# Two transformer blocks on one core: middle chunks of four gated feed-forwards with the weights stationary, and three tiles padded

## Chip, core and metric

The kernel runs on one core of a Trainium2 chip. The metric is the device time of one execution in microseconds (us).

## What is computed

Two blocks work on 256 tokens of width 1024, in float32. The first has an mLSTM mixer and a convolutional gated feed-forward. The second has two layers of three sublayers each: a gated feed-forward, a mixer (gated linear attention, then latent attention), and another gated feed-forward. So block 2 has four gated feed-forwards, each inside a norm before, a norm after and a residual:

```python
D_MODEL = 1024
D_FF = 2816

def swiglu(h, w_gu, w_down):
    gate, up = jnp.split(h @ w_gu, 2, axis=-1)
    return (jax.nn.silu(gate) * up) @ w_down

def sublayer(x, shift, scale, gate, g_pre, g_post, fn, res_weight):
    h = rmsnorm_2(x, g_pre) * (1 + scale[:, None, :]) + shift[:, None, :]
    return x + res_weight * gate[:, None, :] * rmsnorm_2(fn(h), g_post)
```

The vectors `shift`, `scale` and `gate` come from products of a condition vector with large matrices (GEMV), which the kernel does on VectorE.

## The kernel before

All 256 tokens stay on the core: `x` holds two tiles of 128 tokens (a and b). Every matrix product is done in three matmuls. A float32 number is split into a high part (`whi`, `u_hi`, `hh`) and the rest (`wlo`, `u_lo`, `hl`), and `mm3` adds high x high, high x low and low x high into PSUM (L233 to L235). The activations that enter a product, `u_hi` and `u_lo`, have features on partitions, [128, 8, 256].

A *unit* is 512 KB of weights: `unit` loads it into one of 5 `raw` buffers from SyncE's queue, ScalarE casts the high part (L219) and VectorE subtracts to get the low part (L220); 8 places hold each of the two, and some units go to spare places of the arena (`wA`, `wB`, `wC`, `wU`).

A gated feed-forward is cut into 11 chunks of 256 features. `up(c, t)` handles chunk c for token tile t: `as_proj` keeps the activations stationary and streams the weights, 8 steps of three matmuls with 512 columns (256 of the gate, 256 of the value), so its result has tokens on partitions. ScalarE takes Silu (`sg`, L927), VectorE multiplies (`h_`, L929), TensorE transposes the product in two pieces (`pt2`, L932), and `hilo` splits it into `hh` (ScalarE, L228) and `hl` (VectorE, L229). `down(c, t)` multiplies that by two units of the second matrix, 12 matmuls of 512 columns into accumulators of the tile. The four units of an up serve both token tiles. Elsewhere, in the convolutional stage and for keys and queries, `ws_proj` does it the other way round: weights stationary, both token tiles streamed as 256 columns.

What stands in which order: `FFN_ORDER` gives the ups and downs of each feed-forward, one string for each of the four. After each up, `site()` issues as many GEMV slices (`gjunk`, L239, one load of 512 KB each) as the table `FILL` says. A scheduler then orders the instructions of each engine; `urgent` and `pin_b` move the norms between stages ahead and tie units behind them. `modulated` builds the input of a stage out of `xn`: 4 transposes into one PSUM place, scale and shift (`u`, L341 on VectorE for one half, ScalarE for the other), then `u_hi` and `u_lo`.

Tiles of a pool lie one behind another in SBUF. `cols` has 422 floats, 1688 bytes, and the tiles `u_hi` and `u_lo` that follow begin 32 bytes past a multiple of 64; so does one of the arena's places, which follows a tile of 8224 bytes.

Of the kernel before, what the change touches and what calls it, by code (L numbers as in the profile page):

```python
# [18 lines left out]
NF = FF // 128  # L19
# [5 lines left out]
def _cols_layout():  # L25
# [14 lines left out]
# GEMV slices of the modulation vectors issued at each point of the program  # L40
# [7 lines left out]
# chunks of the gated feed-forwards in order: up (u) and down (d), chunk, token tile (a, b)  # L48
FFN_ORDER = (
# [8 lines left out]
)  # L58
# per norm between two stages and token tile: its urgency; weight units and GEMV slices that queue behind it
# [6 lines left out]
# spare places (arena tags) for the weight units of a stage  # L66
# [17 lines left out]
# stages: steps in order  # L84
# [10 lines left out]
def kernel(ctx: ExitStack, tc: tile.TileContext, a: dict, out: bass.AP):  # L95
# [24 lines left out]
    # ---------------------------------------------------------------- constants  # L120
# [12 lines left out]
    cols = const.tile([128, NCOLS], F32, name="cols")  # L133
    nc.sync.dma_start(out=cols, in_=a["cols"])
# [12 lines left out]
    # split activations, features on partitions  # L147
# [3 lines left out]
    def second():  # L151
        """a second stream of split activations: context, then input of the shared keys and values"""
        return [ar.tile([128, 8, 256], F32R, name=f"v{i}", tag=f"U{i}") for i in range(2)]
# [8 lines left out]
    # ---------------------------------------------------------------- helpers  # L162
# [7 lines left out]
    def behind(op, first):  # L170
        """issue op after an earlier instruction of its engine"""
        tc.add_manual_dep(op.ins, first.ins.name, mybir.DependencyInfo(
            mybir.DependencyClass.NoSync, mybir.DependencyReason.DATA), reason="behind a chain")
# [3 lines left out]
    def pin(n, k=0):  # L177
        """the next n weight units queue behind the latest norm"""
        m = dict(mark)
        if k == 1:  # L180
            m["ms"], m["nr"] = m["ehi"], m["elo"]
        elif k == 2:
            m["nr"] = m["elo"]
        elif k == 4:
            m["ms"], m["nr"] = m["xa"], m["xn0"]
        elif k == 3:
            m["ms"] = m["ehi"]
        pins.extend([m] * n)
        return m
# [12 lines left out]
    def ahead(stage, srcs):  # L202
        """the first weight units of the next stage, loaded before their turn"""
        for i, (slot, src) in enumerate(zip("ABC", srcs)):
            early[stage, i] = unit(src, slot)
# [72 lines left out]
    def rsqrt_half(hv, n=1):  # L278
        """hv [128, n] -> 1/sqrt(2 hv): seed from the exponent bits, then Newton steps"""
# [6 lines left out]
        if n == 1:  # L286
            # a step of third order (1.875 - 2.5 t + 1.5 t^2, t = hv y^2), then Newton's
            k = 1.5 ** 0.5
            V.tensor_scalar(out=w[:, 2:3], in0=hv, scalar1=k, scalar2=None, op0=ALU.mult)
            V.scalar_tensor_tensor(out=w[:, 0:1], in0=y, scalar=w[:, 2:3], in1=y, op0=ALU.mult, op1=ALU.mult)  # L290
            V.scalar_tensor_tensor(out=w[:, 1:2], in0=w[:, 0:1], scalar=2.5 / k, in1=w[:, 0:1], op0=ALU.subtract, op1=ALU.mult)
            V.scalar_tensor_tensor(out=r[:, 0:1], in0=w[:, 1:2], scalar=1.875, in1=y, op0=ALU.add, op1=ALU.mult)
            V.scalar_tensor_tensor(out=w[:, 3:4], in0=r[:, 0:1], scalar=hv, in1=r[:, 0:1], op0=ALU.mult, op1=ALU.mult)
            mark["nr"] = V.scalar_tensor_tensor(out=r[:, 1:2], in0=w[:, 3:4], scalar=1.5, in1=r[:, 0:1], op0=ALU.subtract,
                                                op1=ALU.mult, reverse0=True)
            return r[:, 1:2]
# [7 lines left out]
    def mean_square(src, dst, width):  # L304
        """dst [128, 1] = sum(src^2) / (2 width) over the free axis"""
        junk = wk.tile([128, 512], BF16, name="ajunk", tag="ajunk", bufs=1)
        mark["ms"] = S.activation(out=junk[:, :src.shape[-1]], in_=src, func=AF.Square, scale=float(2 * width) ** -0.5, accum_out=dst)  # L307

    def rms_r2(parts, width=D):
        """1/rms over the one or two parts of a row"""  # L310
# [22 lines left out]
    def modulated(xn, gs, sh, uh, ul):  # L333
        """normalised xn [128 tok, 1024] -> split xn * gs + sh, features on partitions"""
# [27 lines left out]
    def t_hilo(src, t):  # L362
        """src [128 tok, 1024] -> u_hi/u_lo[:, :, t]"""
# [5 lines left out]
    def row_of(c):  # L369
        """[128, 8] columns -> [128, 1024] row on every partition"""  # L370
# [21 lines left out]
    def ws_proj(ps, w, uh, ul, nk=8):  # L392
        """weights stationary: ps[128 cols, tokens] = W^T u"""
# [5 lines left out]
    def as_proj(ps, units, n, uh, ul, t):  # L399
        """activations stationary: ps[128 tokens of tile t, n] = u W; units carry 8 k-tiles in order"""  # L400
# [8 lines left out]
    def wo_proj(src, fin, slots=(None,) * 8):  # L409
        """u @ W [1024, 1024], one token tile after the other"""  # L410
# [14 lines left out]
    # ---------------------------------------------------------------- modulation vectors, in order of use  # L425
# [38 lines left out]
    # ================================================================ block 1  # L464
    def cond_rows():
        """c_1 and c_ctx after Silu, on every partition"""
# [8 lines left out]
    def start():  # L475
        """modulated context and latents, keys and gates, one feature tile after the other"""
        b1 = const.tile([128, 8], F32, name="b1")
# [15 lines left out]
        def features(h):  # L493
            """half of the normalised features, on partitions"""
# [33 lines left out]
        def vectors(f):  # L528
            """scale and shift of feature tile f, for context and latents"""
# [21 lines left out]
        def keys(f):  # L551
            """modulated features, their part of the keys and gates"""
# [37 lines left out]
    def mlstm():  # L590
# [4 lines left out]
        # gates, rows: i fwd 0.., i bwd 32.., f fwd 64.., f bwd 96..  # L595
# [53 lines left out]
        # queries, features on partitions  # L649
# [7 lines left out]
        # values and output gates, tokens on partitions  # L657
        vv = [ar.tile([128, 2, H, 257], F32, name=f"vt{i}", tag="BC"[i]) for i in range(2)]
# [22 lines left out]
        # attention  # L681
# [67 lines left out]
    # ---------------------------------------------------------------- conv glu  # L749
    def conv_glu(fin):  # L750
# [9 lines left out]
        def group():  # L760
            """the first feature tiles of gate and value, one token tile after the other"""
# [9 lines left out]
        def tail_val(t):  # L771
            """values of the last feature tiles for token tile t, features on partitions"""
# [122 lines left out]
    # ================================================================ block 2  # L895
# [15 lines left out]
    def swiglu(l, j, after, nxt, hooks):  # L911
        s_ = 0 if j == 0 else 2
        seq = [(e[0], int(e[1:-1]), "ab".index(e[-1])) for e in FFN_ORDER[l * 2 + j].split()]
        W, Wd, hT = {}, {}, {}
# [4 lines left out]

        def up(c, t):  # L920
            if c not in W:
                W[c] = [first(("ffn", l, j), c * 4 + q, a["gu"][l * 2 + j, c, q],
                              EXTRA[c * 4 + q] if c * 4 + q < FFN_FIRST[l * 2 + j] else fs[q] if c == NC - 1 else None) for q in range(4)]
# [13 lines left out]
        def down(c, t):  # L937
            hh, hl = hT.pop((c, t))
# [4 lines left out]
            for k, h in ([(0, 0), (1, 0), (0, 1), (1, 1)] if last else [(0, 0), (0, 1), (1, 0), (1, 1)]):  # L943
                hi, lo = Wd[c][k]
                s = slice(h * 512, h * 512 + 512)
                mm3(acc[t][h], hh[:, k, :], hl[:, k, :], hi[:, s], lo[:, s], cnt[t] == 0 and k == 0, last and k == 1)
# [23 lines left out]
    def gla():  # L970
# [13 lines left out]
        def vr(i, t):  # L984
            """values (i < 2) and output gates, tokens on partitions"""
# [13 lines left out]
        def gates():  # L999
            """cumulative log decay of each chunk"""  # L1000
# [26 lines left out]
        def kq(src, h):  # L1027
            """keys and queries, features on partitions"""
# [107 lines left out]
    def rope(src, dst, tokens, rp):  # L1136
        """src [128, g, tokens] projected pairs of halves -> dst rotated; rp [128, 256] of PSUM"""
# [10 lines left out]
    def mla_u(t, xn):  # L1148
        """modulated input of the shared keys and values, kept until mla_kv"""
# [5 lines left out]
    def mla_latent():  # L1155
        """rotated part of the shared keys, latent of keys and values"""
# [27 lines left out]
    def mla_kn():  # L1184
        """shared keys"""
# [10 lines left out]
    def mla_v():  # L1196
        """shared values"""
# [12 lines left out]
    def mla_mix():  # L1210
# [32 lines left out]
        def latent(t):  # L1243
            """normalised latent of the queries"""
# [16 lines left out]
        def queries(t):  # L1261
            """queries of token tile t, features on partitions: pairs of rotated parts, then heads"""
# [64 lines left out]
def _layout(inp):  # L1327
# [75 lines left out]
    o["gu"] = con(gu.transpose(0, 5, 1, 3, 2, 4, 6)).reshape(4, NC, 4, 128, 1024)  # L1403
# [58 lines left out]
```

## Time and profile before

| what | value |
|---|---|
| median of 3 timed runs | 1444.93 us (1439.31 to 1447.36) |
| profiled execution, span | 1444.4 us |
| TensorE busy | 1395.5 us (97%), 7017 matmuls |
| weight loads busy | 1142.3 us (79%) |
| VectorE busy | 1118.1 us (77%) |
| ScalarE busy | 718.2 us (50%) |
| moved by DMA | 340.06 MB, mean 235 GB/s |

The profiled execution has no timing of its own beside its span, first to last instruction; the median of the timed runs is 0.5 us above it. Busy times overlap between engines. The end of a matmul is modelled in the profile and overlaps with the next one, so the distance between two starts tells what a matmul costs, not its recorded duration.

### The profile page before, as it was taken

Reading aid. Unit: us, or ns where it says so; the run is one execution under the profiler, and the core shown is the slowest. Engines: PE = TensorE matmul, PEld = TensorE weight load, DVE = VectorE, ACT = ScalarE, POOL = GpSimd, SP = SyncE. Lnnn points to the kernel's source line nnn. Section 1 sums busy time; section 2 is a strip of 40 time slices with the busy share of each in tenths; the row PEclk is TensorE's granted clock in tenths of the full one; section 3 lists DMA queues with packets and bytes.
Section 4 is the critical chain, followed back from the end, with each engine's and each line's share of the span. In section 5 each row is a group of like instructions: output and inputs, shape, how many; then the busy total and the mean of one; then the engine's idle time right before and its main releaser. Section 6 shows DMA issues by size and latency. Waiting matters only on the chain.

```text
span 1444.4 us, 19726 instructions
## 1 busy us (share of the span) xinstructions
PE 1395.5 (97%) x7017; PEld 1142.3 (79%) x7017; DVE 1118.1 (77%) x2115; ACT 718.2 (50%) x1188; POOL 18.2 (1%) x42
## 2 busy tenths in 40 slices
PE   7999999999989999999999999999999999999997
PEld 7978877899967888778677788777877887788786
DVE  6887788898688888689787888688878896846563
ACT  4633764545354453566454454563543666644451
POOL 1000000000000000000000000000000000000000
PEclk8999999999999999999999999999999999999999
DMA  8676547797538999668647999559989573447650
GB/s 328 214 263 218 161 150 242 270 317 269 169 116 276 322 338 331 205 219 290 185 148 266 316 341 334 178 155 331 337 281 329 187 235 95 142 159 239 241 189 30
DMA packets 94932, 340.06 MB, mean 235 GB/s; under 512 B 10928, under 2 KB 11248, under 8 KB 94832
## 3 DMA queue, kind: packets, MB, share of 16 engines
q1 hardware_dynamic: 92736, 332.47, 67.4%
q0 software_dynamic: 2096, 6.33, 1.3%
q8 instruction: 55, 0.90, 0.2%
q14 instruction: 45, 0.37, 0.1%
HBM read 337.67 MB, written 1.08 MB: 235 GB/s over the span
## 4 chain that ended last, share of the span: by engine, by line
PE 69%; DVE 11%; DMA 10%; ACT 5%; issue 4%; SPq 0%; DVEq 0%; ACTq 0%; POOLq 0%
PE mm L233 11%; PE mm L234 11%; PE mm L235 11%; PE acc L235 8%; PE acc L233 8%; PE acc L234 8%; DVE wlo L220 3%; DMA raw<-in_cond_w_dram 2%; ACT whi L219 2%; DMA raw<-in_gu_dram 2%; PE acc L715 2%; DVE gjunk L239 2%; PE pt L932 1%; ACT ajunk L307 1%; PE pt L330 1%
## 5 line engine op out<-in xcount | busy, mean ns | idle before, releaser
L220 DVE TENSOR_TENSOR wlo<-raw,whi 128x1024 fp32r<-128x1024 f32 (+1 forms) x385 | 460.1, 1207 | 81.2 <-ACT whi L219 77.3
L219 ACT CAST whi<-raw 128x1024 fp32r<-128x1024 f32 (+1 forms) x385 | 394.1, 1038 | 211.6 <-DMA raw<-in_dn_dram 44.9
L234 PE MATMUL mm<-wlo,u_hi 128*128 128x512 f32 x656 | 261.3, 399 | 0.0
L233 PE MATMUL mm<-whi,u_hi 128*128 128x512 f32 x656 | 260.8, 398 | 0.0
L235 PE MATMUL mm<-whi,u_lo 128*128 128x512 f32 x656 | 259.0, 396 | 0.0
L239 DVE CUSTOM_DVE_ANT_0 gjunk<-raw,c 128x1024 bf16<-128x1024 f32 x192 | 234.4, 1221 | 13.8 <-DMA raw<-in_cond_w_dram 9.5
L233 PE MATMUL acc<-whi,hh 128*128 128x512 f32 x388 | 153.4, 399 | 2.8 <-ACT hh L228 2.8
L235 PE MATMUL acc<-whi,hl 128*128 128x512 f32 x388 | 154.7, 401 | 0.8 <-DVE hl L229 0.8
L234 PE MATMUL acc<-wlo,hh 128*128 128x512 f32 x388 | 154.4, 398 | 0.0
L233 PEld LDWEIGHTS mm<-whi,u_hi 128*128 128x128 f32 x656 | 123.2, 188 | 29.2 <-ACT whi L219 0.4
L235 PEld LDWEIGHTS mm<-whi,u_lo 128*128 128x128 f32 x656 | 123.3, 188 | 28.7
L234 PEld LDWEIGHTS mm<-wlo,u_hi 128*128 128x128 f32 x656 | 123.4, 188 | 28.4 <-DVE wlo L220 0.8
L927 ACT ACTIVATE sg<-mm 128x256 f32<-128x256 f32 x88 | 33.7, 383 | 147.6 <-PE mm L235 147.3
L233 PE MATMUL mm<-u_hi,whi 128*128 128x256 f32 x360 | 102.5, 285 | 0.0
L234 PE MATMUL mm<-u_lo,whi 128*128 128x256 f32 x360 | 102.2, 284 | 0.0
L235 PE MATMUL mm<-u_hi,wlo 128*128 128x256 f32 x360 | 102.0, 283 | 0.0
L233 PEld LDWEIGHTS acc<-whi,hh 128*128 128x128 f32 x388 | 73.5, 190 | 18.3 <-ACT hh L228 3.9
L235 PEld LDWEIGHTS acc<-whi,hl 128*128 128x128 f32 x388 | 73.6, 190 | 17.0 <-DVE hl L229 2.0
L235 PE MATMUL acc<-whi,u_lo 128*128 128x512 f32 (+1 forms) x216 | 86.9, 404 | 0.0
L233 PE MATMUL acc<-whi,u_hi 128*128 128x512 f32 (+1 forms) x216 | 86.6, 402 | 0.0
L234 PE MATMUL acc<-wlo,u_hi 128*128 128x512 f32 (+1 forms) x216 | 86.4, 400 | 0.0
L234 PEld LDWEIGHTS acc<-wlo,hh 128*128 128x128 f32 x388 | 73.5, 190 | 14.8 <-DVE wlo L220 0.6
(733 smaller groups left out, 2152.9 us busy)
## 6 DMA issues: line engine op xcount, KB each, us to landing
raw<-in_gu_dram SPq DMA_DIRECT2D x176, 512.0 KB, 5.0
raw<-in_cond_w_dram SPq DMA_DIRECT2D x144, 512.0 KB, 4.9
raw<-in_dn_dram SPq DMA_DIRECT2D x88, 512.0 KB, 4.8
raw<-in_w_mod_dram SPq DMA_DIRECT2D x32, 512.0 KB, 4.6
raw<-in_f_down_dram SPq DMA_DIRECT2D x22, 512.0 KB, 4.8
raw<-in_f_gate_dram SPq DMA_DIRECT2D x18, 512.0 KB, 4.9
raw<-in_a_vo_dram SPq DMA_DIRECT2D x16, 512.0 KB, 5.2
raw<-in_gl_vr_dram SPq DMA_DIRECT2D x16, 512.0 KB, 5.2
```

Of the source, the lines that this page charges most:

```text
L219: o1 = S.copy(hi[:, :n], r[:, :n])
L220: o2 = V.tensor_tensor(out=lo[:, :n], in0=r[:, :n], in1=hi[:, :n].bitcast(F32), op=ALU.subtract)
L233: T.matmul(ps, lhsT=lh, rhs=rh, start=first, stop=False)
L234: T.matmul(ps, lhsT=lh, rhs=rl, start=False, stop=False)
L235: T.matmul(ps, lhsT=ll, rhs=rh, start=False, stop=last)
L239: return V.tensor_tensor_reduce(out=junk, in0=r, in1=vec, scale=1.0, scalar=0.0, op0=ALU.mult, op1=ALU.add, accum_out=dst)
L307: mark["ms"] = S.activation(out=junk[:, :src.shape[-1]], in_=src, func=AF.Square, scale=float(2 * width) ** -0.5, accum_out=dst)
L330: T.transpose(pt[:, k, :], src[:, (h * 4 + k) * 128:(h * 4 + k + 1) * 128], ident)
L715: T.matmul(np_[:, 0:257], lhsT=w[:, d, s, :], rhs=vt[s][:, h, :], start=(i == 0), stop=(i == len(tiles) - 1))
L927: S.activation(out=sg, in_=ps[:, 0:256], func=AF.Silu)
L932: T.transpose(pt[:, k, :], h_[:, k * 128:k * 128 + 128], ident)
```

## The change

Chunks 2 to 9 of each feed-forward (`WS`) are computed with the weights stationary. `up_ws(f)` handles a tile of 128 features for all 256 tokens: 24 matmuls of 256 columns for the gate and 24 for the value. Its result already has features on partitions, so it is split without transposes. Two such tiles make a chunk; `up(c, t)` with t = 0 and 1 now means the two tiles, each with two units of its own from a new layout `gu_ws`. `down` takes its columns out of both. Chunks 0, 1 and 10 (`ROWWISE`) stay as they were. The four strings are replaced by one sequence for all four feed-forwards. Three tiles (`cols`, `b1`, `vt`) are padded to multiples of 16 floats, so that the tiles behind them begin at multiples of 64 bytes.

```diff
+def LINE(n):
+    return -(-n // 16) * 16
...
+WS = range(2, NC - 1)
+ROWWISE = (0, 1, NC - 1)
+def _ffn_order():
+    seq = [("u", 0, 0), ("u", 1, 0), ("u", 0, 1), ("d", 0, 0), ("u", 1, 1), ("d", 1, 0)]
+    for c in WS:
+        for i in range(2):
+            seq.append(("u", c, i))
+            if c > WS[0]:
+                seq.append(("d", c - 1, i))
+            else:
+                seq.append(("d", i, 1))
+    n = NC - 1
+    return seq + [("u", n, 0), ("d", n - 1, 0), ("d", n, 0), ("u", n, 1), ("d", n - 1, 1), ("d", n, 1)]
...
-    cols = const.tile([128, NCOLS], F32, name="cols")
+    cols = const.tile([128, LINE(NCOLS)], F32, name="cols")
...
-        b1 = const.tile([128, 8], F32, name="b1")
+        b1 = const.tile([128, LINE(8)], F32, name="b1")[:, :8]
...
-        vv = [ar.tile([128, 2, H, 257], F32, name=f"vt{i}", tag="BC"[i]) for i in range(2)]
+        vv = [ar.tile([128, LINE(2 * H * 257)], F32, name=f"vt{i}", tag="BC"[i])[:, :2 * H * 257]
+              .rearrange("p (t h n) -> p t h n", t=2, h=H) for i in range(2)]
...
-        seq = [(e[0], int(e[1:-1]), "ab".index(e[-1])) for e in FFN_ORDER[l * 2 + j].split()]
-        W, Wd, hT = {}, {}, {}
+        seq = FFN_ORDER
+        W, Wd, hT, hF = {}, {}, {}, {}
...
+        def up_ws(f):
+            k = f - 2 * WS[0]
+            wg, wu = [unit(a["gu_ws"][l * 2 + j, k, i]) for i in range(2)]
+            ps = mm_ps()
+            ws_proj(ps[:, 0:256], wg, u_hi, u_lo)
+            ws_proj(ps[:, 256:512], wu, u_hi, u_lo)
+            sg = hp.tile([128, 256], F32, name="sg", tag="sg")
+            S.activation(out=sg, in_=ps[:, 0:256], func=AF.Silu)
+            h_ = hp.tile([128, 256], F32, name="h_", tag="h_")
+            V.tensor_tensor(out=h_, in0=sg, in1=ps[:, 256:512], op=ALU.mult)
+            hF[f] = [ht.tile([128, 256], F32R, name=n, tag=n) for n in ("hh", "hl")]
+            hilo(*hF[f], h_)
...
         def up(c, t):
+            if c in WS:
+                return up_ws(2 * c + t)
...
         def down(c, t):
-            hh, hl = hT.pop((c, t))
+            ts = slice(t * 128, t * 128 + 128)
+            if c in WS:
+                parts = [[v[:, ts] for v in hF[2 * c + k]] for k in range(2)]
+            else:
+                hh, hl = hT.pop((c, t))
+                parts = [(hh[:, k, :], hl[:, k, :]) for k in range(2)]
...
-                mm3(acc[t][h], hh[:, k, :], hl[:, k, :], hi[:, s], lo[:, s], cnt[t] == 0 and k == 0, last and k == 1)
+                mm3(acc[t][h], *parts[k], hi[:, s], lo[:, s], cnt[t] == 0 and k == 0, last and k == 1)
```

How the instructions stand on TensorE in a down of the first feed-forward, before: `acc` are two of the accumulators, `pt` is the transposed product of the up before.

```order
L235 MATMUL acc_4261<-whi,hl 128x512
L233 MATMUL acc_4260<-whi,hh 128x512
L932 MATMUL pt_4596<-ident,h__4594 128x128 x2
L234 MATMUL acc_4260<-wlo,hh 128x512
L235 MATMUL acc_4260<-whi,hl 128x512
L233 MATMUL acc_4261<-whi,hh 128x512
L234 MATMUL acc_4261<-wlo,hh 128x512
```

And the same engine now, at the end of one of the new ups and the start of the down behind it (L250 to L252 are the three lines of `mm3` in the changed file):

```order
L250 MATMUL mm<-u_hi,whi 128x256
L251 MATMUL mm<-u_lo,whi 128x256
L252 MATMUL mm<-u_hi,wlo 128x256
L250 MATMUL acc_4260<-whi,hh 128x512
L251 MATMUL acc_4260<-wlo,hh 128x512
L252 MATMUL acc_4260<-whi,hl 128x512
L250 MATMUL acc_4261<-whi,hh 128x512
L251 MATMUL acc_4261<-wlo,hh 128x512
L252 MATMUL acc_4261<-whi,hl 128x512
```

The transposes inside the down are gone; 48 matmuls of 256 columns and then 12 of 512 follow each other through the middle of the stage.

TensorE at the join of the second and third feed-forward, before: the transposes of `xn` for the second token tile (L330), the first down of the third feed-forward, then the first up of that tile (`mm`).

```order
L330 MATMUL pt<-ident,xn 128x128 x4
L235 MATMUL acc_9051<-whi,hl 128x512
L233 MATMUL acc_9052<-whi,hh 128x512
L234 MATMUL acc_9052<-wlo,hh 128x512
L235 MATMUL acc_9052<-whi,hl 128x512
L233 MATMUL acc_9051<-whi,hh 128x512
L234 MATMUL acc_9051<-wlo,hh 128x512
L233 MATMUL acc_9052<-whi,hh 128x512
L234 MATMUL acc_9052<-wlo,hh 128x512
L330 MATMUL pt<-ident,xn 128x128 x4
L235 MATMUL acc_9051<-whi,hl 128x512
L233 MATMUL mm<-whi,u_hi 128x512
```

And now (L347 are the transposes of `xn`):

```order
L251 MATMUL acc_9723<-wlo,hh 128x512
L252 MATMUL acc_9723<-whi,hl 128x512
L251 MATMUL acc_9724<-wlo,hh 128x512
L252 MATMUL acc_9724<-whi,hl 128x512
L347 MATMUL pt<-ident,xn 128x128 x8
L250 MATMUL mm<-wA,u_hi 128x512
L251 MATMUL mm<-wA,u_hi 128x512
```

The two halves of the transposes have moved together, and the matmuls of the down that lay between them stand ahead of both.

VectorE in the second feed-forward, before (L929 is the product `h_`, L239 a GEMV slice):

```order
L929 TENSOR_TENSOR h__7570<-sg,mm 128x256
L220 TENSOR_TENSOR wlo<-raw,whi 128x1024 x2
L229 TENSOR_TENSOR hl<-pt_7572,hh 128x256
L239 ISA gjunk,mod_118<-raw,c_2574 128x1024
L239 ISA mod_118 128x1
L929 TENSOR_TENSOR h__7614<-sg,mm 128x256
```

And now, in one of the new ups (L237, L246, L256 and L948 are the low half of a unit, `hl`, the slice and the product):

```order
L237 TENSOR_TENSOR wlo<-raw,whi 128x1024
L948 TENSOR_TENSOR h__7894<-sg,mm 128x256
L237 TENSOR_TENSOR wlo<-raw,whi 128x1024
L246 TENSOR_TENSOR hl<-h__7894,hh 128x256
L256 ISA gjunk,mod_118<-raw,c_2574 128x1024
L256 ISA mod_118 128x1
```

`hl` is now taken from the product itself and no longer from the transposed copy in PSUM; a low half of a unit still stands between the two.

## Rows read from the trace of the kernel before

**Rows 1.** The page: busy us of each engine, share of the span, instructions.

```profile
PE 1395.5 (97%) x7017; PEld 1142.3 (79%) x7017; DVE 1118.1 (77%) x2115; ACT 718.2 (50%) x1188; POOL 18.2 (1%) x42
```

**Rows 2.** The page: the chain that ended last, shares by engine.

```profile
PE 69%; DVE 11%; DMA 10%; ACT 5%; issue 4%; SPq 0%; DVEq 0%; ACTq 0%; POOLq 0%
```

**Rows 3.** Windows: convolutional stage, middle of first and last gated feed-forward.

```profile
core 0: us, PE busy (x) PEld busy (x) DVE busy (x) ACT busy (x) POOL busy (x), PEclk, DMA share, GB/s
300.00:400.00 100.00, 99.82 (x691) 92.64 (x690) 77.49 (x124) 44.16 (x62) 0.00 (x0) 1.00 0.72 242
425.00:625.00 200.00, 198.28 (x881) 158.76 (x881) 162.30 (x251) 95.42 (x144) 1.04 (x2) 1.00 0.82 286
1255.00:1435.00 180.00, 178.80 (x794) 143.12 (x793) 99.24 (x132) 75.39 (x109) 1.06 (x2) 1.00 0.53 179
```

**Rows 4.** Waits of TensorE: us in total, times, longest.

```profile
PE pt L932 <- DVE h__10272 L929: 1.1, 1, 1.1
...
PE pt L932 <- DVE h__7614 L929: 0.3, 1, 0.3
PE acc L234 <- DVE wlo L220: 0.3, 1, 0.3
```

**Rows 5.** Timeline of TensorE, last feed-forward: start us, recorded us, instruction.

```profile
1361.69 0.40 PE L233 MATMUL mm<-whi,u_hi 128*128 128x512 f32 x1
...
1367.29 0.40 PE L233 MATMUL acc<-whi,hh 128*128 128x512 f32 x1
...
1368.44 0.38 PE L932 MATMUL pt<-ident,h__12995 128*128 128x128 f32 x2
...
1370.28 0.39 PE L233 MATMUL mm<-whi,u_hi 128*128 128x512 f32 x1
```

**Rows 6.** Timeline of TensorE, convolutional stage.

```profile
343.37 0.28 PE L233 MATMUL mm<-u_hi,whi 128*128 128x256 f32 x1
...
349.07 0.40 PE L233 MATMUL acc<-whi,hh 128*128 128x512 f32 x1
...
351.80 0.28 PE L233 MATMUL mm<-u_hi,whi 128*128 128x256 f32 x1
```

**Rows 7.** Groups of TensorE: count, busy us, mean ns, idle before.

```profile
L233 PE MATMUL mm<-whi,u_hi 128*128 128x512 f32 x656 | 260.8, 398 | 0.0
L233 PE MATMUL acc<-whi,u_hi 128*128 128x512 f32 x204 | 82.5, 405 | 0.0
L233 PE MATMUL mm<-u_hi,whi 128*128 128x256 f32 x360 | 102.5, 285 | 0.0
L233 PEld LDWEIGHTS mm<-u_hi,whi 128*128 128x128 f32 x360 | 69.0, 192 | 1.4 <-ACT u_hi L228 0.2 <-ACT qT L655 0.2
```

**Rows 8.** Timeline of TensorE: 256 columns, tiles at whole lines of 64 bytes.

```profile
1175.41 0.28 PE L234 MATMUL mm<-wlo,qc 128*128 128x256 f32 x1
...
1177.89 0.28 PE L234 MATMUL mm<-wlo,qc 128*128 128x256 f32 x1
...
1188.21 0.28 PE L234 MATMUL mm<-wlo,qc 128*128 128x256 f32 x1
...
1189.46 0.28 PE L233 MATMUL mm<-whi,qc 128*128 128x256 f32 x1
...
1153.61 0.28 PE L233 MATMUL mm<-c_hl,wU 128*128 128x256 f32 x1
...
1154.81 0.29 PE L234 MATMUL mm<-c_hl,wU 128*128 128x256 f32 x1
```

**Rows 9.** Groups of VectorE and ScalarE in the norms between stages.

```profile
L341 DVE TENSOR_SCALAR u<-pt,mod 128x128 f32<-128x128 f32 x64 | 22.4, 403 | 2.3 <-PE pt L330 2.2
L228 ACT CAST u_hi<-u 128x512 fp32r<-128x512 f32 x28 | 17.5, 624 | 17.5 <-DVE u L341 17.3
```

**Rows 10.** Groups of VectorE and ScalarE: unit halves, slice, split of the product.

```profile
L220 DVE TENSOR_TENSOR wlo<-raw,whi 128x1024 fp32r<-128x1024 f32 x368 | 445.1, 1222 | 80.9 <-ACT whi L219 77.1
L239 DVE CUSTOM_DVE_ANT_0 gjunk<-raw,c 128x1024 bf16<-128x1024 f32 x192 | 234.4, 1221 | 13.8 <-DMA raw<-in_cond_w_dram 9.5 <-DMA raw<-in_kv_cond_w_dram 0.9 <-DMA raw<-in_w_mod_dram 0.9
L219 ACT CAST whi<-raw 128x1024 fp32r<-128x1024 f32 x368 | 381.7, 1050 | 211.6 <-DMA raw<-in_dn_dram 44.9 <-DMA raw<-in_gu_dram 36.8 <-PE mm L235 30.6
L228 ACT CAST hh<-pt 128x256 fp32r<-128x256 f32 x88 | 32.7, 371 | 70.3 <-PE pt L932 69.5 <-PE acc L234 0.5
```

More of the change, by code (lines that the diff above doesn't have):

```diff
@@ L47 @@
 )
-FFN_ORDER = (
[8 rows of a table removed]
-)
+WS = range(2, NC - 1)
[11 more added lines that the diff above has]
+    return seq + [("u", n, 0), ("d", n - 1, 0), ("d", n, 0), ("u", n, 1), ("d", n - 1, 1), ("d", n, 1)]
+FFN_ORDER = _ffn_order()
 URGENT = ((300, 1800), (300, 1500), (300, 1500), (1200, 2200), (600, 900), (600, 1800), (600, 1800), (1500, 1500))
@@ L132 @@
     nc.sync.dma_start(out=wsc0, in_=a["w_sc"][0])
-    cols = const.tile([128, NCOLS], F32, name="cols")
-    nc.sync.dma_start(out=cols, in_=a["cols"])
+    cols = const.tile([128, LINE(NCOLS)], F32, name="cols")
+    nc.sync.dma_start(out=cols[:, :NCOLS], in_=a["cols"])
     def col(name, i=0, n=None):
@@ L918, in swiglu @@
         fs = FFN_LAST[l * 2 + j]
+        def up_ws(f):
[10 more added lines that the diff above has]
+            hilo(*hF[f], h_)
         def up(c, t):
+            if c in WS:
+                return up_ws(2 * c + t)
             if c not in W:
-                W[c] = [first(("ffn", l, j), c * 4 + q, a["gu"][l * 2 + j, c, q],
+                W[c] = [first(("ffn", l, j), c * 4 + q, a["gu"][l * 2 + j, ROWWISE.index(c), q],
                               EXTRA[c * 4 + q] if c * 4 + q < FFN_FIRST[l * 2 + j] else fs[q] if c == NC - 1 else None) for q in range(4)]
@@ L1402, in _layout @@
     gu = g["ffn_w_gu_2"].reshape(4, 4, 2, 128, 2, NC, 256)
-    o["gu"] = con(gu.transpose(0, 5, 1, 3, 2, 4, 6)).reshape(4, NC, 4, 128, 1024)
+    o["gu"] = con(gu.transpose(0, 5, 1, 3, 2, 4, 6)[:, list(ROWWISE)]).reshape(4, len(ROWWISE), 4, 128, 1024)
+    gw = g["ffn_w_gu_2"].reshape(4, 8, 128, 2, NF, 128)[:, :, :, :, 2 * WS[0]:2 * WS[-1] + 2]
+    o["gu_ws"] = con(gw.transpose(0, 4, 3, 2, 1, 5)).reshape(4, 2 * len(WS), 2, 128, 1024)
     o["dn"] = con(g["ffn_w_down_2"].reshape(4, NC, 2, 128, 1024))
```

8 rows, old and new, of the table FFN_ORDER are left out of this document.

## The prediction, as made before the result

> **What bounds the kernel now.** I read the page's busy line first: TensorE is busy for 1395.5 of 1444.4 us, VectorE for 1118.1, ScalarE for half [rows 1]. A modelled busy time proves little, so I read the chain that ended last next: 69% of it is TensorE, 11% VectorE, 10% DMA [rows 2]. Then the stages: in the middle of the first and the last gated feed-forward of block 2 TensorE is busy 198.28 of 200 and 178.80 of 180 us at full clock, VectorE only 162.30 and 99.24 [rows 3]. The two stages have very different VectorE and DMA loads and the same TensorE share. So TensorE's own stream is the limit there, and what the change does to the sequence of matmuls is what it is worth, as long as the weights keep coming. Of the waits of TensorE on weights only one of 0.3 us is left in the whole run; the waits inside the middle chunks are for the VectorE product `h_` ahead of a pair of transposes [rows 4].
>
> The recorded duration of a matmul (398 ns for 512 columns [rows 7]) overlaps with the next, so I price by distances between starts. One cycle of a feed-forward, an up and a down, is 8.59 us: 5.60 for the 24 matmuls of the up (1361.69 to 1367.29), 2.99 for the 12 of the down with a pair of transposes in it (to 1370.28) [rows 5].
>
> **The change part by part.** There are 4 stages x 8 middle chunks x 2 = 64 ups that change, and 64 downs that read the new tiles.
>
> *The up.* 24 matmuls of 512 columns and 2 transposes go; 48 matmuls of 256 columns come, with 48 weight loads for 24. The convolutional stage of block 1 already runs this pattern, 48 such matmuls and then 12 of 512: 343.37 to 349.07 is 5.70 us, and to 351.80 another 2.73 [rows 6]. Its whole cycle is 8.43 us against 8.59, 0.16 less. 64 x 0.16 = 10.2 us. If the downs stay as slow as the feed-forward's own (2.99 less the pair, 0.23 by what it adds to 12 x 0.23, gives 2.76 against 2.73), it is 64 x 0.12 = 7.7. I take 9.0.
>
> *The wait for `h_`.* In the change nothing on TensorE waits for `h_`; the first reader is a down that stands a down and a whole next up later. Seven waits of the middle chunks, 1.1 down to 0.3 us, sum to 4.5 [rows 4]; at worst they come back as waits for `hl` (0). I take 4.0. The chain `sg`, `h_`, `hh`, `hl` is four steps of about 0.4 us (`hh` 371 ns [rows 10]), which with a weight half ahead of each (1222 ns on VectorE, 1050 on ScalarE [rows 10]) is 1.6 + 2 x 1.22 + 2 x 1.05 = 6.1 us. The cover is 2.73 + 5.70 = 8.4 us. Without that cover it would cost at least 64 x 1.6 = 102 us.
>
> *ScalarE, VectorE, DMA.* They keep their number of operations; `hh` and `hl` read SBUF instead of PSUM. Bytes and count of the loads are the same (2 units per up for 4 every second up). The cover is their idle time, 38 us of 200 on VectorE and 18% of DMA in the fullest of these stages [rows 3]. I price it at nothing; what it costs if the cover goes is a rival below.
>
> *Padding, stationary side.* `u_hi` and `u_lo` start 32 bytes past a multiple of 64 now, at a multiple after. Remaining 512-column matmuls with u stationary: (656 - 512) + 204 = 348 for each of three lines, 1044 [rows 7]. With u the distance is 5.60 / 24 = 233 ns [rows 5]; with the aligned `hh` it is 2.76 / 12 = 230 in the same stage and 2.73 / 12 = 227.5 in the other [rows 5, 6]. So 0, 3.4 or 6.1 us; I take 3.4, the row of the same stage.
>
> *Padding, moving side.* 64 x 48 new matmuls and 3 x 360 old ones [rows 7], 4152 in all, stream 256 columns. With the misplaced u: 5.70 / 48 = 118.75 ns. Tiles at whole lines show three paces: 21 in 2.48 us (118.1), 11 in 1.25 us (113.6), 10 in 1.20 us (120) [rows 8]. That bounds this term by -21.4 and +5.2 us. The 113.6 appears in one stretch and the 118.1 with the same operands a little earlier, so alignment alone does not give the fast one. I take 118.1: 4152 x 0.65 = 2.7 us.
>
> *The order at a border.* At the join of the second and third feed-forward the 8 transposes of the second token tile now stand together, with the first matmul that needs them right behind; before, 8 matmuls of 0.23 us lay between the two halves. The second half needs the one PSUM place that VectorE empties with 4 x 403 ns, then `u_hi` takes 624 ns [rows 9]: up to 2.2 us that nothing covers, or none if VectorE is done by then. I take 2.0.
>
> *Sum.* 9.0 + 4.0 + 3.4 + 2.7 - 2.0 = 17.1 us off the profiled span of 1444.4: 1427.3. The median of the three timed runs is 1444.93, 0.5 above that span, so the same figure serves for both.
>
> [...] The 48 loads take 192 ns each in the records [rows 7], 9.2 us for an up that lasts 5.70 [rows 6], so loads run beside matmuls and beside each other, and I price the added ones at nothing. [...]
>
> **The rivals.**
> - *Padding does nothing.* Both padding terms are 0: 1444.4 - 11.0 = 1433.4. For it: 118.1 and 118.75 lie within the spread of aligned tiles (113.6 to 120), and 233 against 230 could come from the order of operands. Against it: 227.5 ns in the steadiest stretch.
> - *The fast pace.* The 256-column stream runs at 113.6 ns once u is aligned: 1427.3 + 2.7 - 21.4 = 1408.6. For it: the stretch that shows it. Against: the aligned tiles that don't.
> - *The waits come back.* TensorE is shorter by 0.27 us per up and waits that much for weights or `hl`: 1438 to 1447, no change. For it: ScalarE waits 44.9 and 36.8 us for the transfers of `dn` and `gu` [rows 10], and the transfer share is 0.82 in the first stage [rows 3]. Against: only one wait of TensorE on a weight now, and an up needs two units at once, no longer four.
> - *Slower: weight halves late.* The order of the modulation slices (1.22 us each on VectorE [rows 10]) was kept by up, while the units now come in pairs. Where a slice stands ahead of the second unit of the next up, that up waits for it: 1.2 us for about half of the 64 is 39 us, 1466. It turns the sign from 17.1 / 64 = 0.27 us per up. For it: VectorE is 81% busy in the first stage. Against: in the order of the change most units stand ahead of the product `h_` before the up that needs them.
> - *Slower: bare loads.* If the 24 added loads per up were not hidden, 24 x 0.192 x 64 = 295 us would come on top of 1427: about 1720. Against it: the 5.70 us of the same pattern [rows 6].
>
> **How the numbers follow.** The forecast (1418 to 1437 by its own bounds) has 0.50, padding that does nothing 0.17, the fast pace 0.12, waits that come back 0.13, late halves 0.07, bare loads 0.01. The predicted time is that of the first, 1427. Three runs spread over 8 us, so about 0.5% (7 us) can be told from no change. Faster by more: 0.50 + 0.12 + most of the 0.17 = 0.76; within: 0.13 + the rest = 0.16; slower: 0.08. For 8 in 10 the range reaches half into the fast pace and half into the waits that come back: 1409 to 1440.
>
> **What would show it.** In the profile after: no transposes of `h_` for the middle chunks (48 left of 176); 48 matmuls in about 5.7 us and the next 12 in about 2.75, so a cycle near 8.4; the u-stationary matmuls of chunks 0, 1 and 10 near 230 ns; no wait of TensorE on `wlo`, `whi` or `hl` inside the middle chunks; a wait of some 2 us on `u` at the join of the second and third feed-forward. The prediction is wrong if the cycle is above 8.6 or below 8.2 us, or if the waits on weights add up to more than a few us.

## The result, and the profile after

The changed kernel takes 1433.8 us (1432.3 to 1440.3, six runs), the kernel before 1445.3 beside it; the ratio is 0.9941 with an interval of 0.9916 to 0.9966, so 5 to 12 us less, about 8.5. (The medians lie 11.5 us apart, but single executions of either kernel spread over 8 to 12 us, so the text goes by the ratio and its interval.) The forecast was 1427 us, 17 less. The direction was right and the time lies in the range, but the gain is half of the forecast.

The page of the change (busy us of each engine; then the chain that ended last) looks like that of before [rows 1, 2]: TensorE is busy for 96% of the span, with 1408 matmuls more, and 70% of the chain is still its own.

```profile
PE 1380.0 (96%) x8425; PEld 1204.0 (84%) x8425; DVE 1113.9 (78%) x2115; ACT 720.5 (50%) x1188; POOL 18.2 (1%) x42
PE 70%; DVE 11%; DMA 10%; ACT 4%; issue 3%; SPq 0%; DVEq 0%; ACTq 0%; POOLq 0%
```

The new cycle, in the timeline of TensorE in the last feed-forward (start, recorded us, instruction), answers to [rows 5]:

```profile
1325.51 0.28 PE L250 MATMUL mm<-u_hi,whi 128*128 128x256 f32 x1
...
1331.17 0.40 PE L250 MATMUL acc<-whi,hh 128*128 128x512 f32 x1
...
1333.93 0.28 PE L250 MATMUL mm<-u_hi,whi 128*128 128x256 f32 x1
```

The up takes 1331.17 - 1325.51 = 5.66 us, the down 2.76, the cycle 8.42, where the forecast had 8.43 before padding. So the cycle came. The starts of single Silus say where it paid. In the timeline of ScalarE before (first and last of the first feed-forward, first of the second, second of the third, first and last of the last one):

```profile
428.52 0.38 ACT L927 ACTIVATE sg<-mm 128x256 f32<-128x256 f32 x1 [1.45 <-PE mm L235]
609.58 0.37 ACT L927 ACTIVATE sg<-mm 128x256 f32<-128x256 f32 x1
753.02 0.36 ACT L927 ACTIVATE sg<-mm 128x256 f32<-128x256 f32 x1
953.09 0.38 ACT L927 ACTIVATE sg<-mm 128x256 f32<-128x256 f32 x1 [1.02 <-PE mm L235]
1251.09 0.38 ACT L927 ACTIVATE sg<-mm 128x256 f32<-128x256 f32 x1
1430.38 0.38 ACT L927 ACTIVATE sg<-mm 128x256 f32<-128x256 f32 x1 [3.82 <-PE mm L235]
```

and the same six after:

```profile
427.37 0.39 ACT L961 ACTIVATE sg<-mm 128x256 f32<-128x256 f32 x1 [0.98 <-PE mm L252]
604.86 0.37 ACT L961 ACTIVATE sg<-mm 128x256 f32<-128x256 f32 x1
747.18 0.37 ACT L961 ACTIVATE sg<-mm 128x256 f32<-128x256 f32 x1
942.30 0.39 ACT L961 ACTIVATE sg<-mm 128x256 f32<-128x256 f32 x1 [0.38 <-PE mm L252]
1243.26 0.38 ACT L961 ACTIVATE sg<-mm 128x256 f32<-128x256 f32 x1 [1.31 <-PE mm L252]
1418.54 0.39 ACT L961 ACTIVATE sg<-mm 128x256 f32<-128x256 f32 x1 [4.11 <-PE mm L252]
```

The first feed-forward shrinks from 181.06 to 177.49 us, the last from 179.29 to 175.28: 3.6 and 4.0. The stretch between, from the start of the second to that of the last, holds the second, the third and the mixer behind it, and shrinks from 498.07 to 496.08: 2.0 where two such gains make 7.6. Its first part, up to the second Silu of the third feed-forward, shrinks by 5.0, from 200.07 to 195.12; the rest, that feed-forward and the mixer behind it, grows from 298.00 to 300.96. The loss sits there. Two places show it, both behind the third feed-forward's middle.

The waits of TensorE (us in total, times, longest) have a new one there; the `h_` waits of the middle chunks [rows 4] are gone:

```profile
PE pt L347 <- DVE xn L370: 5.1, 4, 2.4
...
PE pt L966 <- DVE h__11739 L963: 1.2, 1, 1.2
```

`h__11739` is the product of the last chunk (10) of the third feed-forward for the first token tile; that chunk kept its transposes. The longest of the four `xn` waits, 2.43 us, is at the border to the last feed-forward, where the same wait before took 0.72. Windows of that border after (columns as in [rows 3]):

```profile
1228.00:1234.00 6.00, 2.13 (x11) 1.17 (x9) 5.74 (x17) 5.01 (x9) 0.00 (x0) 0.89 0.24 87
1234.00:1240.00 6.00, 5.93 (x17) 4.88 (x18) 5.61 (x16) 5.38 (x14) 0.00 (x0) 0.54 0.01 3
```

and of the same border before:

```profile
1238.00:1244.00 6.00, 3.78 (x19) 2.43 (x17) 5.65 (x17) 5.01 (x9) 0.00 (x0) 1.00 0.32 87
1244.00:1250.00 6.00, 6.00 (x26) 4.68 (x26) 5.83 (x14) 5.69 (x13) 0.00 (x0) 1.00 0.06 10
```

After the longer wait the granted clock is 0.54 of full speed for the next 6 us, in which 17 matmuls start where before it was 26. Before, the clock stayed at 1.00.

The wait at the join of the second and third feed-forward, priced at 2.0, came too. The transposes of the second token tile after, with the first matmul behind them:

```profile
947.25 0.66 PE L347 MATMUL pt<-ident,xn 128*128 128x128 f32 x4
949.37 0.65 PE L347 MATMUL pt<-ident,xn 128*128 128x128 f32 x4 [1.46 <-DVE u L358]
950.02 0.50 PE L250 MATMUL mm<-wA,u_hi 128*128 128x512 f32 x1
```

and the only wait for `u` at the transposes of that tile before:

```profile
959.76 0.66 PE L330 MATMUL pt<-ident,xn 128*128 128x128 f32 x4 [0.23 <-ACT u L345]
```

All waits for `u` at these transposes make 8.6 us, six in number; in the second profile of the change they make 8.4, six too, and in the variants of it 8.5 to 9.5, against 7.2, five in number, before.

### The profile page after: what moved, and what is told of

Same layout as the page of the kernel before. It is cut to its first block, busy times and chain, and to the rows that moved or that the text cites. A ratio compares the mean times of both kernels' runs of the same rounds, so it can differ in the third digit from the quotient of the medians.

```text
span 1432.6 us, 22526 instructions
## 1 busy us (share of the span) xinstructions
PE 1380.0 (96%) x8425; PEld 1204.0 (84%) x8425; DVE 1113.9 (78%) x2115; ACT 720.5 (50%) x1188; POOL 18.2 (1%) x42
## 4 chain that ended last, share of the span: by engine, by line
PE 70%; DVE 11%; DMA 10%; ACT 4%; issue 3%; SPq 0%; DVEq 0%; ACTq 0%; POOLq 0%
PE mm L250 12%; PE mm L252 11%; PE mm L251 11%; PE acc L252 8%; PE acc L250 8%; PE acc L251 8%; DMA raw<-in_cond_w_dram 3%; DVE wlo L237 3%; DVE gjunk L256 2%; PE acc L733 2%; ACT whi L236 1%; ACT ajunk L324 1%; PE pt L347 1%; PE pg L556 1%; DMA row<-d 1%
## 5 line engine op out<-in xcount | busy, mean ns | idle before, releaser
L237 DVE TENSOR_TENSOR wlo<-raw,whi 128x1024 fp32r<-128x1024 f32 (+1 forms) x385 | 462.5, 1207 | 109.6 <-ACT whi L236 106.7
L250 PE MATMUL mm<-u_hi,whi 128*128 128x256 f32 x1384 | 388.5, 281 | 0.2 <-DVE hf L831 0.2
L251 PE MATMUL mm<-u_lo,whi 128*128 128x256 f32 x1384 | 386.6, 279 | 0.0
L252 PE MATMUL mm<-u_hi,wlo 128*128 128x256 f32 x1384 | 386.5, 279 | 0.0
L250 PEld LDWEIGHTS mm<-u_hi,whi 128*128 128x128 f32 x1384 | 260.0, 188 | 4.4 <-DVE hf L831 0.6
L251 PEld LDWEIGHTS mm<-u_lo,whi 128*128 128x128 f32 x1384 | 259.3, 187 | 3.3
L252 PEld LDWEIGHTS mm<-u_hi,wlo 128*128 128x128 f32 x1384 | 260.1, 188 | 0.0
L256 DVE CUSTOM_DVE_ANT_0 gjunk<-raw,c 128x1024 bf16<-128x1024 f32 x192 | 234.3, 1221 | 24.1 <-DMA raw<-in_cond_w_dram 16.5
L250 PE MATMUL acc<-whi,hh 128*128 128x512 f32 x388 | 153.6, 398 | 4.5 <-ACT hh L245 4.5
L252 PE MATMUL acc<-whi,hl 128*128 128x512 f32 x388 | 153.3, 397 | 0.3 <-DVE hl L246 0.3
L252 PEld LDWEIGHTS acc<-whi,hl 128*128 128x128 f32 x388 | 73.4, 189 | 17.4 <-DVE hl L246 0.7
L250 PEld LDWEIGHTS acc<-whi,hh 128*128 128x128 f32 x388 | 72.9, 188 | 17.5 <-ACT hh L245 5.0
L252 PE MATMUL acc<-whi,u_lo 128*128 128x512 f32 (+1 forms) x216 | 86.7, 403 | 0.5 <-DVE u_lo L246 0.5
L250 PE MATMUL acc<-whi,u_hi 128*128 128x512 f32 (+1 forms) x216 | 86.5, 401 | 0.0
L251 PE MATMUL mm<-wlo,u_hi 128*128 128x512 f32 x144 | 57.3, 398 | 0.0
L250 PE MATMUL mm<-whi,u_hi 128*128 128x512 f32 x144 | 57.2, 397 | 0.0
L252 PE MATMUL mm<-whi,u_lo 128*128 128x512 f32 x144 | 57.0, 397 | 0.0
L946 ACT ACTIVATE sg<-mm 128x256 f32<-128x256 f32 x64 | 24.3, 380 | 59.6 <-PE mm L252 59.5
```

The lines of the kernel that those rows point to most:

```text
L237: o2 = V.tensor_tensor(out=lo[:, :n], in0=r[:, :n], in1=hi[:, :n].bitcast(F32), op=ALU.subtract)
L250: T.matmul(ps, lhsT=lh, rhs=rh, start=first, stop=False)
L251: T.matmul(ps, lhsT=lh, rhs=rl, start=False, stop=False)
L252: T.matmul(ps, lhsT=ll, rhs=rh, start=False, stop=last)
L256: return V.tensor_tensor_reduce(out=junk, in0=r, in1=vec, scale=1.0, scalar=0.0, op0=ALU.mult, op1=ALU.add, accum_out=dst)
L946: S.activation(out=sg, in_=ps[:, 0:256], func=AF.Silu)
```

## The experiments

Times are medians in us; the ratio, with its interval in brackets, is that to the kernel before on the same chip. Beside the first four experiments the kernel before takes 1442.6, beside the next four 1442.4, beside the three after them 1442.5.

**Padding alone, and the change without it.** In the first the kernel before gets only this, in the second the change loses it:

```diff
-    cols = const.tile([128, NCOLS], F32, name="cols")
+    cols = const.tile([128, LINE(NCOLS)], F32, name="cols")
...
-        b1 = const.tile([128, 8], F32, name="b1")
+        b1 = const.tile([128, LINE(8)], F32, name="b1")[:, :8]
```

(and `vt` in the same way).

> The kernel before with only the three tiles padded; all ups still with the activations stationary. Here 2580 matmuls of 512 columns have u stationary and 1080 of 256 columns stream it. As priced in the prediction: 2580 x 3 ns and 1080 x 0.65 ns, 8.4 us less, about 1436.5, and the 24 matmuls of an up at 5.52 us instead of 5.60. By what the profile of the change shows (24 such matmuls in 5.58 us at the median, 48 of 256 columns in 5.66 for 5.70): 0.8 ns and 0.8 ns each, about 3 us less, 1442. If padding does nothing: 1445 and 5.60 us.

> The change without the three padded tiles. As priced in the prediction: 1044 x 3 ns + 4152 x 0.65 ns, 6.1 us slower than the change, about 1440, ups of 48 matmuls at 5.70 us and downs at 2.76. By the profile of the change: 4152 x 0.83 ns and 1044 x 0.8 ns, 4.3 us, of which downs at 2.74 instead of 2.76 would give back up to 1.6: 1436 to 1438. If padding does nothing: 1434 and a cycle of 8.42 us.

Padding alone: 1441.1, ratio 0.9993 (0.9979 to 1.0008), no change that can be told. The median of 23 stretches of 24 matmuls of 512 columns, with no wait and nothing else in them, is 5.60 us as before; 48 of 256 columns take 5.66 for 5.70. The change without padding: 1437.5, ratio 0.9967 (0.9955 to 0.9978), with ups of 5.70 and downs of 2.74, a cycle of 8.44; the change beside it 1434.2, 0.9948. So padding is worth some 3 us in the change, half of the priced 6.1; the two intervals overlap, so the times alone do not settle it. The traces do show it: padding makes an up 0.04 us shorter and a down 0.02 longer. The stationary side, priced at 3 ns a matmul, shows 5.58 for 5.60 us per 24 in the change (under 1 ns a matmul) and nothing in the old order.

**The same two kernels once more.** No edit; another profile of each.

> The changed kernel once more, for another profile. If the long row (6.30 us) and the half clock at the border to the last feed-forward belong to the order of the change, they stand here too, and the span is 1432 to 1434. If they are an accident of one execution, the row lands in 4.8 us as before, the clock stays full there, and the span is near 1428 to 1430.

> The kernel before once more, for another profile. If the border to the last feed-forward runs clean in the old order (row of the gate in 4.8 us, TensorE at full clock), the profile shows that again. If that was an accident of the first profile, as the profile with the padding alone suggests (TensorE waits up to 2.6 us for xn and a clock of 0.81 and 0.85 in the two slices there), the wait and the lower clock stand here too.

The change again: 1434.2, ratio 0.9948 (0.9930 to 0.9966). At the border the norm needs the gate row, the row that scales the mixer's result; its load took 6.56 us (6.30 in the first profile), the `xn` wait was 2.9, and the granted clock from 1230 to 1240 was 0.68: as in the first profile (0.66). Before again: span 1440.4; the row took 5.38, the `xn` wait at the border 1.2, the clock of the two slices of 10 us there was 0.97 and 0.86. So in the old order the border is not always clean, and the first profile (4.78, 0.7 and full clock) was its better side. From the second feed-forward's first Silu to the last one's: 495.4 before and 498.1 after. Over both profiles of each, that stretch gained nothing (496.8 to 497.1); the part from the third feed-forward's second Silu on lost 4.6 (297.3 to 301.9).

**The gate row earlier.** The gate row of the last mixer goes through DRAM and back. It is issued ahead of the attention of the first token tile now, in the change and in the kernel before:

```diff
+            if step == "a0":
+                coef = row_of(mod2[:, 14, :])
             steps[step[0]](*[int(x) for x in step[1:]])
...
-        coef = row_of(mod2[:, 14, :])
```

> The change with the gate row of the last mixer made ahead of the attention of the first token tile instead of behind that of the second. If the late row is what holds TensorE at the border to the last feed-forward (the trace of the change: the row took 6.30 us to land, TensorE waits 2.43 us for xn and then runs 5 us at half clock, where before the row took 4.78 us, the wait was 0.72 and the clock stayed full): VectorE starts the norm up to 6 us earlier, the wait and the slow stretch go, 3 to 5 us less, about 1430. If the norm is held by something else there, or the wait was only that execution's: no change, 1434.

> The kernel before with the gate row of the last mixer made ahead of the attention of the first token tile, as in the change with the same edit (which won 0.2%). If the late row holds TensorE in the old order too, and the first profile only escaped it: 2 to 3 us less than before, 1440. If the change brought that wait: within 1 us of before.

In the change 1431.3, 0.9928 (0.9913 to 0.9942), 2.9 us less than the change beside it, though the intervals overlap; the `xn` wait at the border falls to 0.3 us and the clock there is full (0.989 as the mean of the run, for 0.986 in the change). In the kernel before 1440.0, 0.9982 (0.9970 to 0.9993), 2.6 us less. So the late row holds both orders on the average: it explains the slow stretch in the profile, not why the change won too little. But the profile of the change with the early row shows the other place at its worst. Its timeline of VectorE and TensorE at the end of the third feed-forward:

```profile
1114.31 1.23 DVE L237 TENSOR_TENSOR wC<-raw,wC 128x1024 fp32r<-128x1024 f32 x1 [0.50 <-ACT wC L236]
1115.73 1.22 DVE L237 TENSOR_TENSOR wlo<-raw,whi 128x1024 fp32r<-128x1024 f32 x1 [0.19 <-ACT whi L236]
1116.87 0.41 DVE L963 TENSOR_TENSOR h__11739<-sg,mm 128x256 f32<-128x256 f32 x1
...
1117.34 0.69 PE L966 MATMUL pt<-ident,h__11739 128*128 128x128 f32 x2 [3.01 <-DVE h__11739 L963]
```

The product stands behind two low halves on VectorE, which wait for ScalarE's high halves, and those for their loads. TensorE waits 3.01 us, and from 1118 to 1123 the clock is 0.77. The same wait was 1.21 and 1.99 us in the two profiles of the change, with full clock behind it, and 2.08 without padding, with a clock of 0.67 from 1120 to 1125.

**The loads behind that wait.** ScalarE in the first profile of the change, around the Silu of that last chunk (the units here, `whi` and `wC`, belong to the two downs of the end, which have four; the first of them is cast at 1110.85):

```profile
1112.11 1.05 ACT L236 CAST whi<-raw 128x1024 fp32r<-128x1024 f32 x1
1113.31 1.05 ACT L236 CAST wC<-raw 128x1024 fp32r<-128x1024 f32 x1 [0.16 <-DMA raw<-in_dn_dram]
1114.65 1.05 ACT L236 CAST whi<-raw 128x1024 fp32r<-128x1024 f32 x1 [0.29 <-DMA raw<-in_dn_dram]
1115.60 0.38 ACT L961 ACTIVATE sg<-mm 128x256 f32<-128x256 f32 x1
```

and before:

```profile
1127.52 1.05 ACT L219 CAST whi<-raw 128x1024 fp32r<-128x1024 f32 x1 [1.24 <-DMA raw<-in_dn_dram]
1129.58 0.38 ACT L927 ACTIVATE sg<-mm 128x256 f32<-128x256 f32 x1 [1.01 <-PE mm L235]
1129.86 1.04 ACT L219 CAST wC<-raw 128x1024 fp32r<-128x1024 f32 x1
1132.39 1.05 ACT L219 CAST whi<-raw 128x1024 fp32r<-128x1024 f32 x1
```

Before, the Silu waits for the matmuls alone (1.01 us on `mm`), and two of the four down units come behind it. In the new order all four stand ahead of it on the same engine, so a Silu that needs no load starts only behind the last cast, which has waited for its load. Those loads end a long row on SyncE's queue in the change (start, us, load; `cond_w` are slices of the modulation vectors, `gu` the four units of chunk 10):

```profile
1087.34 1.80 SPq L182 DMA_DIRECT2D raw<-in_gu_ws_dram  x2
1090.29 7.75 SPq L182 DMA_DIRECT2D raw<-in_cond_w_dram  x6
1099.06 4.34 SPq L182 DMA_DIRECT2D raw<-in_gu_dram  x4
1104.55 5.07 SPq L182 DMA_DIRECT2D raw<-in_dn_dram  x4
```

Six slices stand ahead of the eight units that this end needs, 7.75 us of a queue that is full. (Before, it was eight slices at this place, but two units less had to be there for the Silu.) How full, windows of the change say: the middle of the first and of the third feed-forward, and the last stretch before that Silu (the share of DMA is the last number but one):

```profile
460.00:580.00 120.00, 120.00 (x858) 112.78 (x857) 101.39 (x142) 58.59 (x77) 1.04 (x2) 1.00 0.94 342
980.00:1100.00 120.00, 119.67 (x862) 112.28 (x861) 98.64 (x154) 56.24 (x79) 2.15 (x4) 1.00 0.90 323
1110.00:1115.00 5.00, 5.00 (x23) 4.05 (x22) 4.05 (x6) 3.71 (x5) 0.00 (x0) 1.00 0.94 332
```

and the middle of the third before:

```profile
980.00:1100.00 120.00, 117.83 (x555) 95.16 (x554) 99.45 (x159) 55.38 (x79) 2.15 (x4) 1.00 0.90 319
```

From 1085 to 1115 the share is 0.94 to 1.00 in every 5 us. But a full queue alone does not make the loss: the first feed-forward, with 0.94 in its middle, won all of its share.

The next edit moves the six slices from behind the last middle chunk to two places earlier in that feed-forward. It is one row of the table:

```diff
-    4, 0, 1, 0, 3, 1, 2, 2, 4, 2, 6, 0, 0, 0, ...
+    4, 3, 1, 3, 3, 1, 2, 2, 4, 2, 0, 0, 0, 0, ...
```

It is tried with the early row, alone (twice, the second time beside 1444.5 for the kernel before), and in the kernel before.

> The change with the early row, and six slices of the modulation vectors moved from behind the last middle chunk of the third feed-forward to two earlier places in it. With the early row alone TensorE waits 3.0 us for h_ of the last chunk there, behind low halves of weights whose loads come late, and then runs at half clock. If the slices (512 KB and 1.2 us of VectorE each) are what makes those loads late: that wait falls below 1 us, with the slow stretch behind it 2 to 4 us less than with the early row alone, 1428 to 1429. If the loads are late for another reason, the wait stays and the time is 1431.

> The change with the six slices moved earlier and the gate row where it was. If the wait for the last chunk's h_ in the third feed-forward and the late row are two separate losses, this wins what the slices won on top of the early row (3.3 us): 1430 to 1431, with the wait for the row left in the profile. If one only uncovers the other, it wins less than 1 us: 1433 to 1434.

> The kernel before with the same six slices moved. In its three profiles TensorE loses 0.9 to 2.0 us around the end of the third feed-forward, against 1.1 to 4.8 in those of the change. If the slices are late only for the new order of the units, this is within 1 us of before, 1442. If they hold the old order too: 2 to 3 us less, and the change has no loss of its own there.

> The change with the six slices moved and the gate row where it was, once more. In its first profile the row was there by 4.7 us and held nobody; in the three profiles of the change's order with the slices in their old place (with and without padding) it took 6.17 to 6.56 us. If the slices' place decides that too, the row lands within 5 us again, the stretch from the end of the third feed-forward to the last one loses some 23.5 us again instead of 26 to 28, and the time is 1429. If the first profile was lucky: 6 us or more, a wait for xn above 2 us, and the time still 1429 to 1431 by the wait for h_ that is gone.

With the early row 1427.9, 0.9895 (0.9878 to 0.9912). Alone 1429.3, 0.9902 (0.9879 to 0.9926), and again 1428.8, 0.9898 (0.9868 to 0.9928). In the kernel before 1444.9, 1.0018 (1.0002 to 1.0033): 2.6 us slower. So the place of these slices is worth some 6 to 7 us in the new order (0.9941 and 0.9948 to 0.9902 and 0.9898; by the intervals about 3 to 10), and the old place is right for the old order. The two losses are not separate: without the early row the border is clean too, where a wait for the row was expected. From the profile of the slices moved alone (first of the two): the Silu of chunk 10, the `xn` waits of TensorE in the whole run (at this border it is 0.29), and the windows at the border:

```profile
1113.87 0.39 ACT L961 ACTIVATE sg<-mm 128x256 f32<-128x256 f32 x1 [3.81 <-PE mm L252]
PE pt L347 <- DVE xn L370: 2.8, 4, 1.3
```

```profile
1222.00:1228.00 6.00, 5.71 (x27) 4.16 (x25) 4.85 (x15) 5.44 (x9) 0.00 (x0) 1.00 0.19 57
1228.00:1234.00 6.00, 4.49 (x21) 3.31 (x21) 5.61 (x18) 5.18 (x15) 0.00 (x0) 1.00 0.09 33
```

The Silu waits for matmuls alone again, no wait for `h__11739` is left, the clock is full, and VectorE starts the norm 4.7 us after the row was issued, behind a matmul and no longer behind the row. The stretch from the second feed-forward to the last is 492.1 and 490.9 us for 497.1, its part from the second Silu of the third on 296.8 and 295.7 for 301.9. Why the row lands sooner when slices far ahead of it stand elsewhere is not settled. Nor was the place of the casts ahead of the Silu tried by itself; that it makes the slices' place matter is read from the rows.

**No transposes.** The kernel before without the two transposes of the middle chunks:

```diff
-            pt = ps_tr.tile([128, 2, 128], F32, name="pt2", tag="tr")
-            for k in range(2):
-                T.transpose(pt[:, k, :], h_[:, k * 128:k * 128 + 128], ident)
+            pt = h_.rearrange("p (k n) -> p k n", k=2)
+            if c in (0, 1, NC - 1):
+                (as before)
```

> The kernel before without the transposes of h_ in the middle chunks: the split reads h_ itself, so its output is another one. It keeps 24 matmuls of 512 columns and all waits of the split on h_. If the transposes and their waits are what the change wins, each pair gives 0.22 us and the seven waits 4.5 us: a cycle of 5.60 + 2.76 = 8.36 us, 14 to 19 us less than before, 1424 to 1429, and more than the change won, since its 48 matmuls take 0.06 longer. If their time is taken up elsewhere (the waits come back, now for hl), 8 us less or below, 1435 or more.

It takes 1430.6, 0.9909 (0.9892 to 0.9926), 13 us less, a little short of the 14 to 19. Twenty-four matmuls still take 5.60 us and a down 2.77 at the median. Other waits came up, for a low half of a unit (2.2 us in two). So the transposes and their waits are the prize; the new form of the matmuls costs 0.06 us an up (5.66 for 5.60) and wins nothing by itself.

**The old end of the third feed-forward.** On top of early row and moved slices, the down of chunk 9 for the second tile stands ahead of the last up, in that feed-forward alone:

```diff
+        seq = list(FFN_ORDER)
+        if (l, j) == (1, 0):
+            seq[-3], seq[-2] = seq[-2], seq[-3]
```

> The change with early row and moved slices, and in the third feed-forward the old end: the down of chunk 9 for the second token tile ahead of the last up instead of behind it. In the profiles with the early row TensorE loses 22 to 24 us from the end of that feed-forward to the start of the last one in the new order, 20 in the old. If the new end of the sequence brings that (work of the mixer left uncovered): 1 to 3 us less, 1425 to 1427. If not: 1428, and the reason stays open.

It takes 1426.4, 0.9887 (0.9865 to 0.9909), against 0.9895: the intervals overlap, and it can't be told from no gain. In its profile the stretch from the second to the last feed-forward is 489.8 us (490.9 without the edit). It is the lowest time of all; whether the edit has a share in that is open.

## Why the prediction was half right

- **What bounds the kernel.** TensorE's stream does in the first and the last feed-forward: each won 3.5 us or more in both profiles of the change. In the third one, and the mixer behind it, the order of loads took that gain away. The prediction read a DMA share of 0.82 off the whole first feed-forward [rows 3], whose middle has 0.93; the third, where the loss came, it did not look at.
- **The up.** Forecast 9.0 less, from 8.59 to 8.43. Without padding the cycle is 8.44, 64 x 0.15 = 9.6. Right. The 48 loads of an up take 188 ns each in the records of the change, 9.0 us in sum, and the up takes 5.66: they stay hidden.
- **The wait for `h_`.** The seven waits of the middle chunks went. Their 4.5 us come from one profile; the second profile of the kernel before has 2.1 us in such waits, so the 4.0 was on the high side. What the prediction left out is that chunk 10 keeps its transposes: its wait grew to 1.2 us, in other profiles of the change's order to 2.0 to 3.0, twice with a slower clock behind it. So a part was given back, by the rival that waits come back (0.13), at one place instead of at every up.
- **ScalarE, VectorE, DMA at nothing.** This step failed. The cover named for it was the mean idle time of a stage, 18% of DMA; at the end of the third feed-forward the DMA share is 0.94 to 1.00 and ScalarE waits for loads. The rival "weight halves late" had the mechanism (a slice ahead of a unit, the table kept by up) but looked for it in the middle chunks, at 1.2 us each. It sits where the pairs end: six slices, four units of chunk 10, four of the downs, and the Silu behind them. It is worth 6 to 7 us in place of nothing, shown by moving the slices; the same move costs the old order 2.6, so this loss is the change's own.
- **Padding.** This term was mis-sized: 2.8 for 6.1. Of the 3.4 for the stationary side the 1044 matmuls, 43.5 times 24, gave 43.5 x 0.02 = 0.9. The 233 against 230 ns was not the start of `u`, as the 5.60 us with padding alone shows; the difference of operands that the rival named is left, untested. The moving side gave 0.83 ns for 0.65, 4152 of them 3.5 us. The slower downs, some 80 by estimate, took 80 x 0.02 = 1.6 back. The two ratios give 2.7. That the start of a tile moves the pace rests on these runs alone: the 5.70 against 5.66 us speaks for it in a small way, the 5.60 in the old order, with and without padding, against it.
- **The join.** 2.0 was priced; TensorE waits 1.46 us there for `u`. The wait came as described, and the price was 0.5 too high.
- **The sum.** 17.1, less 3.3 for padding, and 0.5 back for the join, makes 14.3. With the slices moved the change has 14.1 and 14.7. With the slices where they were it is 14.3 less 6 to 7, so 7 to 8, and the two measurements of the change gave 8.5 and 7.5. The sums agree no better than the intervals and the term for `h_` allow, 2 us or so. The time of 1433.8 is the figure of the rival "padding does nothing", 1433.4, but that is luck: padding did something, and the rest was lost elsewhere.

## What to carry to other kernels

The shorter stream on the busiest engine was worth its price here only where the loads arrived in time: it gave 8.5 and 7.5 us with the six slices in their old place, 14.1 and 14.7 with them moved. When a change alters how many units a step takes, follow the loads and the casts in their order through the steps that did not change, next to those that did, and read the DMA share of that place and not of a whole stage. A table that was kept from the old order is part of the change; here one row of it held nearly half of the gain. Two waits of TensorE cost more here than their own length: behind those of 2.43 and 1.52 us at the border only 17 matmuls started in 6 us at a granted clock of 0.54, where 26 did at 1.00.

## What the hardware showed that was not expected

A wait of 2.43 us and one of 1.52 close behind, with 11 matmuls around them, were followed by a granted clock of 0.54 for 6 us; waits of 0.72 and 1.50 at the same border left it at 1.00, and 1.21 and 1.52, in the second profile of the kernel before, were followed by 0.72 for 6 us. Padding sped up the ups (5.70 to 5.66) and slowed the downs (2.74 to 2.76); which of the three tiles does which was not tried. A broadcast of 4 KB to all partitions out of DRAM took 4.78 to 6.56 us at one and the same place of the program.
